# Eight of sixteen ff2 chunks in seven half products, with part of the weight sums made in memory

## The chip, the core and the metric

The kernel runs on one core of a Trainium2 chip. TensorE (PE in the profile; PEld is its weight load) multiplies into PSUM, VectorE (DVE) and ScalarE (ACT) do elementwise work on SBUF and PSUM, GpSimd (POOL) does little here, and SyncE (SP) issues nearly all loads from memory. Each engine works through its own queue in order and waits on semaphores for what others make. The metric is the device time of one execution in microseconds, as the median of some runs.

## The reference

One decoder layer on a sequence of 256 tokens of 1024 channels, in float32. What matters here is its second half:

```python
mixed = g_nsa * (y_nsa @ w_up_nsa[layer]) + g_moba * (y_moba @ w_up_moba[layer])
x = x + mixed @ w_out[layer]                 # 1024 x 1024

h2 = rmsnorm(x, norm2_g[layer])
u = jax.nn.relu(h2 @ w_ff1[layer])           # 1024 x 4096
x = x + (u * u) @ w_ff2[layer]               # 4096 x 1024
return rmsnorm(x, norm_f_g)
```

Ahead of it stand a norm, one wide input projection and two attention mixers.

## The kernel before

**Chunks and slots.** All weights are cut into 60 chunks of up to 1 MB (128 rows of 2048 floats), in the list CHUNKS: kva/kvb (0 to 3), q, qm, km, vm (4 to 11), gm (12 to 19), upn and upm (20 to 23), wout (24 to 27), ff1 (28 to 43), ff2 (44 to 59). The kernel goes through them in slots, one for each chunk. A slot is a list of matmuls with other engines' work put at places in it: `at(pos, f, ...)` notes f at a share of the slot, and `run_slot` calls it ahead of the matmul at that share. So a place only sets the order in which instructions enter their queues; when one runs is up to its engine's queue and to its data.

**Two halves of every number.** Products are made in a fast format, so every operand is split into a rounded part (hi) and a rest (lo), and a product is three matmuls: hi by hi, hi by lo, lo by hi (`mm3`). `split` makes both halves of a weight chunk: ACT copies to hi (L114), DVE subtracts for lo (L116). It runs two slots ahead of its use; loads (`load`, L95) run up to five ahead into three raw buffers, and each waits until the last reader of its buffer's former chunk is done. There are also three hi and three lo buffers, so a chunk's hi waits until PE is through with the slot three chunks before.

**wout.** Each slot makes two blocks of 128 output channels from eight input blocks k (`two_blocks`, 48 matmuls of 256 columns). In the first slot the inputs k = 4 to 7 come late: `mix_t` transposes them on PE into a bank of PSUM, ACT copies them to mxh (L746), `mix_l` lets DVE make mxl (L750). So the slot first does k = 0 to 3 for both blocks, then 4 to 7, always three matmuls for one k.

**ff1.** Sixteen slots of the same form. `ff1_evac` takes a slot's result from PSUM: relu on ACT, the square on DVE (L937), its rounded copy on ACT (L938) and the rest on DVE (L939), into sqh and sql.

**ff2.** Chunk i has the weights of 256 of the 4096 inner channels (two blocks k) for all 1024 outputs. A plain slot is 24 matmuls of 512 columns: two halves of the tokens (t), two blocks k, two halves of the outputs, three matmuls each, added up in four banks of PSUM (`ops`). The chunks in SEVEN (2, 4, 6, 8, 10, 12) are done in the manner of Strassen and Winograd: as 2 by 2 blocks, with seven products in place of eight, 21 matmuls (`seven_mms`). That needs sums of blocks: of the activations (`s_sums`, `s_split`, in ff1) and of the weights (`t_sums`, four subtractions on DVE in place in the raw buffer, L913; then `t_hi`, L920, and `t_lo`, L924, which split the four sums T). Products that enter several outputs (P1, P5, P6, P7) have banks of their own, and `seven_sum` adds them into x1 in the last slots. `x1_rows` turns the layer's residual from columns to rows with 16 transposes on PE, in ff2's slot 1. The last slot does chunks 14 and 15 and puts out the result by `final_a` and `final_b`.

**Queues.** SP issues all loads in the order of the calls. POOL has sixteen small operations at the start, up to the norm's power (L229, L230), and two at the very end (L1048); it issues no transfer.

Of the kernel before, what the change touches and what calls it, by code (L numbers as in the profile page):

```python
# [41 lines left out]
def hybrid_layer(ctx: ExitStack, tc: tile.TileContext, firstd, gxd, w, w1c, small, const, gf, out):  # L42
# [59 lines left out]
    def split(c, part, parts=2, which=""):  # L102
        if c >= NCH:
            return
        n = CHUNKS[c][2]
# [4 lines left out]
        if seven(c):  # L110
            a, b = ((0, 512), (1024, 2048))[part]
        v = raw[c][:, a:b] if c else raw0[:, part]
        if which != "l":
            act.activation(hi[c][:, a:b], v, AF.Copy)  # L114
        if which != "h":
            dve.tensor_tensor(lo[c][:, a:b], v, hi[c][:, a:b].bitcast(F32),  # L116
                              op=ALU.subtract)
# [4 lines left out]
    for _ in range(7):  # L122
        pe.matmul(warm[:, 0:128], zero, zero, start=True, stop=True, skip_group_check=True)
    ident = cp.tile([128, 128], F32, name="ident")
    make_identity(nc, ident)
# [517 lines left out]
    for sec, c0, n in groups:  # L643
# [244 lines left out]
    def s_sums(i, r):  # L888
        if not SS:
            FB["p"].tile([128, 40], F32, name="gap3")  # L890
            for n, e in (("h", 128), ("l", 16)):
                SS[n] = cp.tile([128, 2048 + e], F32R, name="s" + n, tag="act" + n.upper())
                SS[n + "x"] = FB["p"].tile([128, 384], F32R, name="sx" + n)
        j = SEVEN.index(i)
        for n in "hl":
            SS[i, n] = (SS[n][:, 16 + 384 * j:400 + 384 * j] if j < 5 else SS[n + "x"])
# [2 lines left out]
        for o, x, y, op in ((0, A[1][0], A[1][1], ALU.add), (2, A[0][0], A[1][0], ALU.subtract),
                            (1, S[0], A[0][0], ALU.subtract), (3, A[0][1], S[1], ALU.subtract)):  # L900
            dve.tensor_tensor(S[o], x, y, op=op)
# [7 lines left out]
    def t_sums(c):  # L909

        b = raw[c].rearrange("p (a n) -> p a n", a=4)
        for o, x, y in ((0, 1, 0), (1, 3, 1), (3, 3, 0), (2, 2, 3)):
            dve.tensor_tensor(b[:, o], b[:, x], b[:, y], op=ALU.subtract)  # L913

    def t_hi(c, a):
        if a == 0:
            for n in "hl":
                TT[n] = FB["p"].tile([128, 2176 if n == "h" else 2096], F32R, name="t" + n, tag="h2" + n)[:, 0:2048]
        v = slice(1024 * a, 1024 * a + 1024)
        act.activation(TT["h"][:, v], raw[c][:, v], AF.Copy)  # L920

    def t_lo(c, a):
        v = slice(1024 * a, 1024 * a + 1024)
        dve.tensor_tensor(TT["l"][:, v], raw[c][:, v], TT["h"][:, v].bitcast(F32),  # L924
                          op=ALU.subtract)


    def ff1_evac(i, outs, whole):
# [6 lines left out]
        else:  # L935
            act.activation(rf, whole, AF.Relu)
        dve.tensor_tensor(rf, rf, rf, op=ALU.mult)  # L937
        act.activation(h, rf, AF.Copy)  # L938
# [65 lines left out]
    def seven_sum():  # L1004

        s1 = scr[:, 0:512]
        u2, u3 = (FB["p"].tile([128, 2, 256], F32, name="ur", bufs=2)
                  .rearrange("p a q -> p (a q)") for _ in range(2))
        r0, r1 = fst[:, 4:5], fst[:, 5:6]
        add = lambda o, v, r: dve.scalar_tensor_tensor(o, v, r, o, op0=ALU.mult, op1=ALU.add)  # L1010
        act.activation(s1, PP["P1"], AF.Copy)
        dve.tensor_tensor(u2, PP["P6"], s1, op=ALU.add)
        dve.tensor_tensor(u3, PP["P7"], u2, op=ALU.add)
        add(x1[:, 0, 0:512], s1, r0)
        add(x1[:, 0, 512:1024], u2, r0)
        add(x1[:, 0, 512:1024], PP["P5"], r0)
        add(x1[:, 1].rearrange("p (a n) -> p a n", a=2),
            u3[:, None, :].to_broadcast([128, 2, 512]), r1)
        add(x1[:, 1, 512:1024], PP["P5"], r1)

# [43 lines left out]
    for i in range(15):  # L1064
        c = C_FF2 + i
        if i == 13:
            split_events(c, (0.0, 0.1), (0.1, 0.2))
            at(0.45, seven_sum)
        else:
            std_events(c)  # L1070
        for f, a in prev:
            at(0.02, f, *a)
        prev = []
        if i + 2 in SEVEN:
            at(0.62, t_sums, c + 2)
            at(0.65, t_hi, c + 2, 0)
            at(0.66, t_hi, c + 2, 1)
        if i + 1 in SEVEN:
            for a in range(2):
                at(0.03, t_lo, c + 1, a)  # L1080
            at(0.04, load, c + 4)
# [112 lines left out]
```

## Time and profile before

| what | value |
|---|---|
| three runs | 376.36, 376.53, 376.57 us; median 376.53 |
| the profiled execution's own time | 376.16 us |
| its span, first to last instruction | 374.2 us |
| granted TensorE clock, mean | 0.996 |
| DVE's weight splits (L116), 124 of them | 136.3 us busy |
| ACT's weight splits (L114), 124 of them | 118.7 us busy |
| DVE's sums of weight blocks (L913), 24 of 128x512 | 16.6 us busy, 690 ns each |
| DVE's rests of these sums (L924), 12 of 128x1024 | 14.6 us busy, 1221 ns each |
| ff loads, 32 of 1024 KB | 4.9 us from issue to landing (median) |

The profile is of one execution. Its page lists for each engine the busy time, the chain of work that ended last, groups of like instructions (busy time, mean duration in ns, idle time before them and who ended it) and the loads. Matmuls overlap, so the mean duration of one is longer than the spacing between two. The span leaves out 1.96 us of the execution's time, at its start and end.

### The profile page before, as it was taken

The page shows a single profiled execution, that of the slowest core. Times are in us where ns is not written, and L with a number is a line of the kernel's source. Part 1 is how long each engine was busy: PE and PEld are TensorE (multiplying, and loading weights), DVE is VectorE, ACT ScalarE, POOL GpSimd, SP SyncE. Part 2 cuts the span into 40 slices and gives each one's busy share as a digit, 9 for nine tenths or more (in the row PEclk, how much of TensorE's full clock was granted, in tenths as well). Part 3 has the DMA queues.
Part 4 walks back from the last instruction along what each step waited for, and adds up shares of the span by engine and source line. Part 5 has one row for each costly group of instructions (what it writes and reads, how often), then busy time and mean ns, then how long its engine had stood idle before and what let it go on. Part 6 is the DMA issues. An engine that isn't in the chain of part 4 may idle for free.

```text
span 374.2 us, 6013 instructions
## 1 busy us (share of the span) xinstructions
PE 365.3 (98%) x2388; PEld 321.1 (86%) x2388; DVE 295.5 (79%) x476; ACT 220.0 (59%) x382; POOL 6.6 (2%) x18
## 2 busy tenths in 40 slices
PE   8989999999999999999999999999999999999993
PEld 8977778878888788778999999999998888888883
DVE  5878888896966869766867688787778879999685
ACT  6876465767747667344455566766664785555412
POOL 3020000000000000000000000000000000000000
PEclk9999999999999999999999999999999999999998
DMA  7996445334533335550675656456655535655202
GB/s 244 394 412 228 134 177 205 112 114 126 194 130 115 112 119 200 152 203 2 222 286 176 200 190 213 158 192 226 207 160 198 207 131 165 234 199 202 99 0 112
DMA packets 11259, 66.89 MB, mean 179 GB/s; under 512 B 1248, under 2 KB 2272, under 8 KB 3936
## 3 DMA queue, kind: packets, MB, share of 16 engines
q1 hardware_dynamic: 10800, 65.61, 50.1%
q10 hardware_dynamic: 432, 0.92, 0.7%
q8 instruction: 18, 0.29, 0.3%
q14 instruction: 9, 0.07, 0.1%
HBM read 65.47 MB, written 1.05 MB: 178 GB/s over the span
## 4 chain that ended last, share of the span: by engine, by line
PE 83%; DVE 7%; ACT 3%; DMA 3%; issue 2%; SPq 1%; POOL 1%; POOLq 0%; ACTq 0%; DVEq 0%
PE acc L253 53%; PE o L253 13%; PE P L253 4%; PE qacc L253 3%; PE yb L253 2%; DVE wlo L116 2%; DMA raw<-in_kvb_dram 2%; ACT whi L114 2%; DMA g0x<-in_first_dram 1%; DVE x L1010 1%; PE Sa L551 1%; PE Sb L551 1%; PE Sa L253 1%; PE Sb L253 1%; PE tp L341 1%
## 5 line engine op out<-in xcount | busy, mean ns | idle before, releaser
L114 ACT ACTIVATE whi<-raw 128x1024 fp32r<-128x1024 f32 (+3 forms) x124 | 118.7, 984 | 53.3 <-PE acc L253 33.8
L116 DVE TENSOR_TENSOR wlo<-raw,whi 128x1024 fp32r<-128x1024 f32 (+3 forms) x124 | 136.3, 1130 | 13.1 <-ACT whi L114 13.0
L253 PE MATMUL acc<-h2h,whi 128*128 128x256 f32 x256 | 70.7, 276 | 0.0
L253 PE MATMUL acc<-h2l,whi 128*128 128x256 f32 x256 | 70.7, 276 | 0.0
L253 PE MATMUL acc<-h2h,wlo 128*128 128x256 f32 x256 | 70.7, 276 | 0.0
L253 PE MATMUL acc<-whi,hTh 128*128 128x512 f32 (+1 forms) x128 | 50.4, 399 | 0.5 <-ACT whi L114 0.3
L253 PE MATMUL acc<-wlo,hTh 128*128 128x512 f32 (+1 forms) x128 | 49.7, 393 | 0.0
L253 PE MATMUL acc<-whi,hTl 128*128 128x512 f32 (+1 forms) x128 | 49.1, 389 | 0.0
L253 PEld LDWEIGHTS acc<-h2h,whi 128*128 128x128 f32 x256 | 48.0, 188 | 0.0
L253 PEld LDWEIGHTS acc<-h2l,whi 128*128 128x128 f32 x256 | 48.0, 188 | 0.0
L253 PEld LDWEIGHTS acc<-h2h,wlo 128*128 128x128 f32 x256 | 48.0, 188 | 0.0
L253 PE MATMUL o<-whi,sqh 128*128 128x512 f32 (+1 forms) x86 | 33.1, 385 | 0.0
L253 PE MATMUL o<-whi,sql 128*128 128x512 f32 (+1 forms) x86 | 33.0, 384 | 0.0
L253 PE MATMUL o<-wlo,sqh 128*128 128x512 f32 (+1 forms) x86 | 33.0, 384 | 0.0
L253 PEld LDWEIGHTS acc<-whi,hTh 128*128 128x128 f32 x128 | 24.1, 190 | 6.9 <-issue 1.3
L253 PEld LDWEIGHTS acc<-whi,hTl 128*128 128x128 f32 x128 | 24.3, 190 | 4.3
L253 PEld LDWEIGHTS acc<-wlo,hTh 128*128 128x128 f32 x128 | 24.3, 190 | 3.8
L920 ACT ACTIVATE th<-raw 128x1024 fp32r<-128x1024 f32 x12 | 12.8, 1063 | 19.2 <-DVE raw L913 19.2
L939 DVE TENSOR_TENSOR sql<-ur,sqh 128x512 fp32r<-128x512 f32 x16 | 11.1, 692 | 11.2 <-ACT sqh L938 11.2
L253 PEld LDWEIGHTS o<-whi,sql 128*128 128x128 f32 x86 | 16.2, 188 | 3.2
L253 PEld LDWEIGHTS o<-wlo,sqh 128*128 128x128 f32 x86 | 16.1, 188 | 3.2
L253 PEld LDWEIGHTS o<-whi,sqh 128*128 128x128 f32 x86 | 16.2, 188 | 3.1
(319 smaller groups left out, 643.1 us busy)
## 6 DMA issues: line engine op xcount, KB each, us to landing
raw<-in_ff_dram SPq DMA_DIRECT2D x32, 1024.0 KB, 4.9
raw<-in_gm_dram SPq DMA_DIRECT2D x8, 1024.0 KB, 4.8
raw<-in_wout_dram SPq DMA_DIRECT2D x4, 1024.0 KB, 5.0
raw<-in_q_dram SPq DMA_DIRECT2D x2, 1024.0 KB, 7.2
raw<-in_qm_dram SPq DMA_DIRECT2D x2, 1024.0 KB, 7.5
raw<-in_km_dram SPq DMA_DIRECT2D x2, 1024.0 KB, 5.6
raw<-in_vm_dram SPq DMA_DIRECT2D x2, 1024.0 KB, 4.9
raw<-in_upn_dram SPq DMA_DIRECT2D x2, 1024.0 KB, 4.9
```

Of the source, the lines that this page charges most:

```text
L114: act.activation(hi[c][:, a:b], v, AF.Copy)
L116: dve.tensor_tensor(lo[c][:, a:b], v, hi[c][:, a:b].bitcast(F32), op=ALU.subtract)
L253: pe.matmul(o, l, r, start=start, stop=stop, skip_group_check=True)
L341: pe.transpose(tp[:, j * 256 + t * 128:j * 256 + t * 128 + 128], src[:, t, (2 * i + j) * 128:(2 * i + j + 1) * 128], ident)
L551: pe.transpose(S[x][:, j, c:c + 128], P[:, 2 * x + j, c:c + 128], ident)
L920: act.activation(TT["h"][:, v], raw[c][:, v], AF.Copy)
L939: dve.tensor_tensor(l, rf, h.bitcast(F32), op=ALU.subtract)
L1010: add = lambda o, v, r: dve.scalar_tensor_tensor(o, v, r, o, op0=ALU.mult, op1=ALU.add)
```

## The change

- SEVEN becomes (1, 2, 4, 5, 7, 8, 10, 11): eight chunks, in four pairs of neighbours with a plain one between pairs.
- The blocks of these chunks' weights are stored in another order, so that the three blocks that are used as they are (B) are the first 1536 columns; only these are loaded by `load`, 768 KB.
- Of the four weight sums T, two are now made in memory: POOL issues for each such chunk a copy of two blocks into a tile in memory (`v_copy`) and a transfer that adds the fourth block to both (`v_add`), noted in slots 7 to 22 at 0.6. `v_load` (SP, 512 KB) brings the two sums into SBUF, into two buffers vv. DVE makes the other two with two additions (`t_sums`).
- T's hi and lo have one buffer for all of ff2. `t_hi` and `t_lo` of a second chunk of a pair fill its first half at 0.72 of the first chunk's slot, its second half at the start of their own slot.
- The products run in the order P1, C11, C12, P5, P7, P6, C21 (P5, P7, P6, C21 first before).
- Loads of ff2, splits and sums get new places; `seven_sum` is cut in two, in slots 12 and 13; `x1_rows` moves to ff1's slot 3 and uses ff2's four banks.
- In `ff1_evac` ACT makes both squares, and DVE's multiplication goes.
- In wout's first slot (`kinds`), k = 4 to 7 are done kind by kind: all hi by hi, all lo by hi, then all hi by lo. The second `mix_t` there moves from 0.29 to 0.25.

```diff
-SEVEN = (2, 4, 6, 8, 10, 12)
+SEVEN = (1, 2, 4, 5, 7, 8, 10, 11)
...
     def load_part(c, i, parts, m=1):
         sec, j, n = CHUNKS[c]
+        n = 1536 if seven(c) else n
...
+    def v_copy(i):
+
+        VD[i] = dp.tile([128, 1024], F32, name=f"vd{i}")
+        b = w["ff2"][i].rearrange("p (a n) -> p a n", a=4)
+        pool.dma_start(VD[i].rearrange("p (a n) -> p a n", a=2), b[:, 0:3:2, :])
+
+    def v_add(i):
+        b = w["ff2"][i].rearrange("p (a n) -> p a n", a=4)
+        pool.dma_start(VD[i].rearrange("p (a n) -> p a n", a=2),
+                       b[:, 3:4, :].to_broadcast([128, 2, 512]), accum_op=ALU.add)
+
+    def v_load(i):
+        VS[i] = FB["p"].tile([128, 1024], F32, name="vv", bufs=2)
+        nc.sync.dma_start(VS[i], VD[i])
...
+    def v_events(c):
+
+        j = c - 7
+        if 0 <= j < 2 * len(SEVEN):
+            at(0.6, (v_copy, v_add)[j % 2], SEVEN[j // 2])
...
-                mms += wstat(outs[m], c, m * 128, 8, 256, ah, al, ks=ks, last=7)
+                if not (kinds and ks[0]):
+                    mms += wstat(outs[m], c, m * 128, 8, 256, ah, al, ks=ks, last=7)
+        if kinds:
+            for w, x, end in ((hi, ah, 8), (lo, ah, 8), (hi, al, 7)):
+                for m in range(2):
+                    for k in range(late, 8):
+                        mms.append(lambda o=outs[m], w=w[c][:, k * 256 + m * 128:k * 256 + m * 128 + 128],
+                                   x=x[:, k, :], z=k == end: mm(o, w, x, False, z))
...
-            at(0.29, lambda: mix_t(1, 1, s_tile(1)[:, 0]))
+            at(0.25, lambda: mix_t(1, 1, s_tile(1)[:, 0]))
...
-        b = raw[c].rearrange("p (a n) -> p a n", a=4)
-        for o, x, y in ((0, 1, 0), (1, 3, 1), (3, 3, 0), (2, 2, 3)):
-            dve.tensor_tensor(b[:, o], b[:, x], b[:, y], op=ALU.subtract)
+        b = raw[c][:, 0:2048].rearrange("p (a n) -> p a n", a=4)
+        dve.tensor_tensor(b[:, 2], b[:, 2], VS[c - C_FF2][:, 0:512], op=ALU.add)
+        dve.tensor_tensor(b[:, 1], b[:, 1], b[:, 2], op=ALU.add)
+
+    def t_src(c, a):
+        return raw[c][:, 512:1536] if a else VS[c - C_FF2]
...
-        dve.tensor_tensor(rf, rf, rf, op=ALU.mult)
-        act.activation(h, rf, AF.Copy)
+        act.activation(h, rf, AF.Square)
+        act.activation(rf, rf, AF.Square)
         dve.tensor_tensor(l, rf, h.bitcast(F32), op=ALU.subtract)
...
+        if i == 3:
+            at(0.5, x1_rows, range(4), [FB["o"].tile([128, 512], F32, name=f"o{t}_{a}")
+                                        for t in range(2) for a in (0, 512)])
+        if i in (9, 11):
+            at(0.6, v_load, SEVEN[(i - 9) // 2])
...
-        for name, a, b in (("P5", S[0], T[0]), ("P7", S[2], T[1]), ("P6", S[1], T[3]),
-                           ("C21", sq(1, 1), T[2]), ("P1", sq(0, 0), B[0]),
-                           ("C11", sq(0, 1), B[2]), ("C12", S[3], B[3])):
+        for name, a, b in (("P1", sq(0, 0), B[0]), ("C11", sq(0, 1), B[1]), ("C12", S[3], B[2]),
+                           ("P5", S[0], T[0]), ("P7", S[2], T[1]), ("P6", S[1], T[3]),
+                           ("C21", sq(1, 1), T[2])):
...
+        S0, S1, S2 = (i + k in SEVEN for k in range(3))
         if i == 13:
             split_events(c, (0.0, 0.1), (0.1, 0.2))
-            at(0.45, seven_sum)
+        elif S0:
+            split_events(c, *(((0.1, 0.45), (0.4, 9)) if S1 else ((0.4, 0.5), (0.5, 0.6))))
         else:
-            std_events(c)
+            split_events(c, (0.3, 0.45), (0.4, 0.5))
+        if S0:
+            at(0.0, t_hi, c, 1)
+            at(0.01, t_lo, c, 1)
+            at(0.03, load, c + 3)
+            if not S1:
+                at(0.035, load, c + 4)
+            n = SEVEN.index(i) + 2
+            if n < len(SEVEN):
+                at(0.04, v_load, SEVEN[n])
+        if S1:
+            at(0.2 if S0 else 0.1, t_sums, c + 1)
+            at(0.72 if S0 else 0.15, t_hi, c + 1, 0)
+            at(0.73 if S0 else 0.16, t_lo, c + 1, 0)
+        if i in (SEVEN[-1] + 1, SEVEN[-1] + 2):
+            at(0.5, seven_sum, i - SEVEN[-1] - 1)
         for f, a in prev:
             at(0.02, f, *a)
-        prev = []
...
+        prev = [(split, (c + 2, 1, 2, "l"))] if S0 and S1 else []
...
-        if i == 1:
-            at(0.5, x1_rows, range(4), [acc_tile() for _ in range(3)] + [bank("yb", "yb")])
...
+    for i in SEVEN:
+        d["ff2"][i] = d["ff2"][i].reshape(128, 4, 512)[:, [0, 2, 3, 1]].reshape(128, 2048)
```

More of the change, by code (lines that the diff above doesn't have):

```diff
@@ L110, in split @@
         if seven(c):
-            a, b = ((0, 512), (1024, 2048))[part]
+            a, b = ((0, 512), (512, 1536))[part]
         v = raw[c][:, a:b] if c else raw0[:, part]
@@ L297, in split_events @@
                 at(ls[i], split, c + 2, i, 2, "l")
-        if ls[1] <= 1 and not seven(c + 2):
+        if ls[1] <= 1 and not seven(c + 2) and not seven(c + 1):
             at(max(ls) + 0.05, load, c + 5)
@@ L665, in hybrid_layer @@
             unit_events(c)
+            v_events(c)
             if c == 5:
@@ L780, in hybrid_layer, with two_blocks @@
             prev = [(evac, (1, i, accs[1]))]
-    def two_blocks(c, ah, al, late=8):
+    def two_blocks(c, ah, al, late=8, kinds=False):
         if late < 8:
@@ L868, in hybrid_layer @@
         else:
-            mms, outs, _ = two_blocks(c, mxh, mxl, 4 if i == 0 else 8)
+            mms, outs, _ = two_blocks(c, mxh, mxl, 4 if i == 0 else 8, i == 0)
             run_slot(mms)
@@ L892, in s_sums @@
                 SS[n] = cp.tile([128, 2048 + e], F32R, name="s" + n, tag="act" + n.upper())
[L893 removed]
+                SS[n + "x"] = FB["p"].tile([128, 384 * (len(SEVEN) - 5)], F32R, name="sx" + n)
         j = SEVEN.index(i)
         for n in "hl":
[L896 removed]
+            SS[i, n] = (SS[n][:, 16 + 384 * j:400 + 384 * j] if j < 5 else
+                        SS[n + "x"][:, 384 * (j - 5):384 * (j - 4)])
         S = [FB["scr"][:, 128 * a:128 * a + 128] for a in range(4)]
         A = [[r[:, k, 128 * t:128 * t + 128] for k in range(2)] for t in range(2)]
[L899 to L900 removed]
+        for o, x, y, op in ((0, A[1][0], A[1][1], ALU.subtract), (2, A[0][0], A[1][0], ALU.subtract),
+                            (1, S[0], A[0][0], ALU.subtract), (3, A[0][1], S[1], ALU.add)):
             dve.tensor_tensor(S[o], x, y, op=op)
@@ L909, in t_sums @@
     def t_sums(c):
-        b = raw[c].rearrange("p (a n) -> p a n", a=4)
-        for o, x, y in ((0, 1, 0), (1, 3, 1), (3, 3, 0), (2, 2, 3)):
-            dve.tensor_tensor(b[:, o], b[:, x], b[:, y], op=ALU.subtract)
+        b = raw[c][:, 0:2048].rearrange("p (a n) -> p a n", a=4)
[3 more added lines that the diff above has]
+        return raw[c][:, 512:1536] if a else VS[c - C_FF2]
     def t_hi(c, a):
-        if a == 0:
+        if not TT:
             for n in "hl":
                 TT[n] = FB["p"].tile([128, 2176 if n == "h" else 2096], F32R, name="t" + n, tag="h2" + n)[:, 0:2048]
-        v = slice(1024 * a, 1024 * a + 1024)
-        act.activation(TT["h"][:, v], raw[c][:, v], AF.Copy)
+        act.activation(TT["h"][:, 1024 * a:1024 * a + 1024], t_src(c, a), AF.Copy)
     def t_lo(c, a):
         v = slice(1024 * a, 1024 * a + 1024)
-        dve.tensor_tensor(TT["l"][:, v], raw[c][:, v], TT["h"][:, v].bitcast(F32),
+        dve.tensor_tensor(TT["l"][:, v], t_src(c, a), TT["h"][:, v].bitcast(F32),
                           op=ALU.subtract)
@@ L1002, in seven_mms, with seven_sum @@
         return r
-    def seven_sum():
+    UU = {}
+    def seven_sum(t):
+        add = lambda o, v, r: dve.scalar_tensor_tensor(o, v, r, o, op0=ALU.mult, op1=ALU.add)
         s1 = scr[:, 0:512]
[L1007 to L1019, printed above, removed]
+        if t == 0:
+            UU[2], UU[3] = (FB["p"].tile([128, 2, 256], F32, name="ur", bufs=2)
+                            .rearrange("p a q -> p (a q)") for _ in range(2))
+            act.activation(s1, PP["P1"], AF.Copy)
+            dve.tensor_tensor(UU[2], PP["P6"], s1, op=ALU.add)
+            dve.tensor_tensor(UU[3], PP["P7"], UU[2], op=ALU.add)
+            dve.tensor_tensor(UU[2], PP["P5"], UU[2], op=ALU.subtract)
+            add(x1[:, 0, 0:512], s1, fst[:, 4:5])
+            add(x1[:, 0, 512:1024], UU[2], fst[:, 4:5])
+        else:
+            add(x1[:, 1, 0:512], UU[3], fst[:, 5:6])
+            dve.tensor_tensor(UU[3], PP["P5"], UU[3], op=ALU.subtract)
+            add(x1[:, 1, 512:1024], UU[3], fst[:, 5:6])
     def final_a(p, j):
@@ L1065, in hybrid_layer @@
         c = C_FF2 + i
+        S0, S1, S2 = (i + k in SEVEN for k in range(3))
         if i == 13:
             split_events(c, (0.0, 0.1), (0.1, 0.2))
-            at(0.45, seven_sum)
-        else:
-            std_events(c)
+        elif S0:
+            split_events(c, *(((0.1, 0.45), (0.4, 9)) if S1 else ((0.4, 0.5), (0.5, 0.6))))
+        else:
+            split_events(c, (0.3, 0.45), (0.4, 0.5))
[14 more added lines that the diff above has]
+            at(0.5, seven_sum, i - SEVEN[-1] - 1)
         for f, a in prev:
             at(0.02, f, *a)
-        prev = []
[L1074 to L1081, printed above, removed]
+        prev = [(split, (c + 2, 1, 2, "l"))] if S0 and S1 else []
         if i == SEVEN[0]:
```

6 lines of the change are left out of this document (5 added, 1 removed).

## The prediction

> **What bounds the kernel now.** I read the page's busy shares first, then the chain of work that ended last, then the waits of PE, then busy time by stretch.
>
> ```profile
> span 374.2 us, 6013 instructions
> PE 365.3 (98%) x2388; PEld 321.1 (86%) x2388; DVE 295.5 (79%) x476; ACT 220.0 (59%) x382; POOL 6.6 (2%) x18
> PE 83%; DVE 7%; ACT 3%; DMA 3%; issue 2%; SPq 1%; POOL 1%; POOLq 0%; ACTq 0%; DVEq 0%
> ...
> PE yb L123 <- PEq L1178: 0.8, 1, 0.8
> PE tp L253 <- DVE xsq L222: 0.7, 1, 0.7
> PE acc L253 <- ACT whi L114: 0.3, 1, 0.3
> PE tp L388 <- ACT kcd L318: 0.3, 1, 0.3
> PE yb L742 <- DVE sga L735: 0.3, 1, 0.3
> PE acc L253 <- DVE kml L360: 0.2, 1, 0.2
> PE acc L253 <- DVE mxl L750: 0.2, 1, 0.2
> ...
> 177.00:283.00 106.00, 106.00 (x936) 106.00 (x936) 83.24 (x124) 63.51 (x89) 0.00 (x0) 1.00 0.60 204
> 283.00:356.00 73.00, 73.00 (x332) 60.67 (x331) 62.63 (x71) 43.29 (x51) 0.00 (x0) 1.00 0.49 173
> ```
>
> PE holds 83% of the chain, and its seven waits come to 2.8 us in all. The two stretches (columns: length, busy time of PE, PEld, DVE, ACT, POOL, granted clock, DMA share, GB/s) hold three of the four wout slots, the ff1 stage and the ff2 stage to its last slot: PE never pauses there and its clock is full. So in these stages one matmul less is its full price less, as long as DVE (86% in the second stretch), ACT and the loads still deliver in time.
>
> The price of a matmul is not its mean duration:
>
> ```profile
> L253 PE MATMUL o<-whi,sqh 128*128 128x512 f32 x82 | 32.0, 390 | 0.0
> ...
> 176.81 106.25 PE acc L253 x935
> ...
> 299.13 6.80 PE o L253 x30
> ```
>
> By the groups one 512-column matmul lasts 390 ns; by the chain, 30 of them take 6.80 us, so one starts every 0.2267 us; the 256-column ones follow each other at 106.25/935 = 0.1136 us. I take the spacing. [...]
>
> **The change, part by part.**
>
> *Eight chunks instead of six.* A plain ff2 chunk is 24 matmuls, a seven chunk 21. Two more seven chunks remove 6 x 0.2267 = 1.36 us of PE, in the second stretch, where nothing hides them. Moving the 16 transposes of x1_rows from ff2 slot 1 to ff1 slot 3 costs PE the same in either place: 0.
>
> *wout's first slot by kinds.* One wait of PE lies there:
>
> ```profile
> 176.38 0.28 PE L253 MATMUL acc<-mxh,whi 128*128 128x256 f32 x1
> 176.81 0.39 PE L253 MATMUL acc<-mxl,whi 128*128 128x256 f32 x1 [0.15 <-DVE mxl L750]
> 177.03 0.28 PE L253 MATMUL acc<-mxh,wlo 128*128 128x256 f32 x1
> ...
> 175.43 0.60 ACT L746 ACTIVATE mxh<-Sb 128x512 fp32r<-128x512 f32 x1
> 176.06 0.69 DVE L750 SCALAR_TENSOR_TENSOR mxl<-Sb,mxh 128x512 fp32r<-128x512 f32 x1 [0.87 <-ACT mxh L746]
> ```
>
> The first late matmul needs only mxh (there at 176.03) and starts on time; the next needs mxl, which ends at 176.75. Starts are 0.43 and 0.22 us apart where 0.113 is normal: 0.32 + 0.11 = 0.43 us lost, of which I take 0.42. By kinds, sixteen matmuls that need no mxl come first (16 x 0.1136 = 1.8 us), so the first reader of mxl stands at about 178.2, 1.4 us after mxl is ready. mix_t's second call is put two matmuls of 48 earlier; mxh still follows the ACT split before it (174.37 to 175.42), so it is not earlier and need not be. Gain 0.42 us. PE is then that much ahead of DVE, whose next work is the wlo of wout's second slot: from 176.75, 2.35 us (two such splits, in a row below), first half ready at 177.9, second at 179.1. That slot starts at 176.38 + 24 x 0.1136 = 179.1 and reads the second half twelve matmuls in, at 180.5: no new wait.
>
> *ff1's evacuation.* DVE's multiplication goes, ACT gets a second square:
>
> ```profile
> L937 DVE TENSOR_TENSOR ur<-ur 128x512 f32<-128x512 f32 x16 | 11.0, 690 | 7.7 <-ACT ur L936 6.7 <-ACT ur L934 1.0
> L938 ACT ACTIVATE sqh<-ur 128x512 fp32r<-128x512 f32 x16 | 10.1, 633 | 14.7 <-DVE ur L937 14.7
> L906 ACT ACTIVATE sh<-fscr 128x384 fp32r<-128x384 f32 x5 | 2.6, 527 | 1.8 <-DVE fscr L901 1.8
> L906 ACT ACTIVATE sqh<-fscr 128x128 fp32r<-128x128 f32 x6 | 1.9, 311 | 0.4
> ```
>
> A 512-wide ACT operation takes 0.63 here, and I price relu, squares and row copies alike by it. An ff1 slot on PE is 48 x 0.1136 = 5.45 us. ACT has two splits (1.99, in the next fence) + 3 x 0.63 + 0.31 + 0.53 (s_split) = 4.7 us. Slot 3 also gets four row copies (2.5): ACT runs some 1.8 us late there, and its splits are made two slots ahead of PE. Cost 0; without that lead it would be those 1.8 us, once. The two more s_sums and s_splits lie on DVE and ACT in slots with room: 0.
>
> *ff2 in pairs.* Seven chunks now come as (1,2), (4,5), (7,8), (10,11), with one lasting buffer for the T blocks. The rows for DVE and ACT:
>
> ```profile
> 286.18 1.82 DVE L116 TENSOR_TENSOR wlo<-raw,whi 128x512 fp32r<-128x512 f32 x2
> 287.92 2.86 DVE L913 TENSOR_TENSOR raw<-raw 128x512 f32<-128x512 f32 x4
> 290.69 2.44 DVE L924 TENSOR_TENSOR tl<-raw,th 128x1024 fp32r<-128x1024 f32 x2
> 293.05 2.35 DVE L116 TENSOR_TENSOR wlo<-raw,whi 128x1024 fp32r<-128x1024 f32 x2
> ...
> 289.36 1.06 ACT L920 ACTIVATE th<-raw 128x1024 fp32r<-128x1024 f32 x1 [2.87 <-DVE raw L913]
> 291.78 1.99 ACT L114 ACTIVATE whi<-raw 128x1024 fp32r<-128x1024 f32 x2
> ```
>
> Before, two slots (10.2 us of PE) hold 1.82 + 2.86 + 2.44 + 2.35 = 9.47 us of DVE, 93%. After, t_sums has two operations (1.43) instead of four; a group of three slots (2 x 4.76 + 5.44 = 14.96 us) holds 2 x (1.82 + 1.43 + 2.44) + 2.35 = 13.7 us, 92%. No tighter on the mean, so order decides. I count from the start of a pair's first slot, products at 3 x 0.2267 = 0.68 us each in the new order P1, C11, C12, P5, P7, P6, C21. The second chunk's first T half overwrites what P5 and P7 read, so ACT's t_hi waits for P7's end at 3.4 (and the matmul's own length, some 0.2): it runs 3.6 to 4.7, t_lo on DVE 4.7 to 5.9. The second slot's P5 reads it at 4.76 + 2.04 = 6.8: 0.9 us spare. The other half waits for C21 (4.9), is ready at about 7.2, and P6 reads it at 8.2: 1.0 spare. Queued on DVE ahead of them are t_lo (1.2), t_sums (1.4) and a split (1.1), over by about 3.6. In the first pair, where DVE still has the last ff1 evacuation, t_lo ends at about 6.5 against 6.8: 0.2 to 0.3 spare, the tightest place. At the end, seven_sum's first half (five 512-wide operations of 0.69, 3.5 us of DVE) now stands ahead of the last chunk's lo split; by the same count that split ends some 0.9 us before its reader. Cost 0; a miss in any of these places costs PE what it is late by.
>
> *Loads.* A seven chunk now brings 768 KB and 512 KB of sums' parts instead of 1 MB.
>
> ```profile
> raw<-in_ff_dram SPq DMA_DIRECT2D x32, 1024.0 KB, 4.9
> q1 hardware_dynamic: 10800, 65.61, 50.1%
> ...
> raw<-in_ff_dram SPq DMA_DIRECT2D x1, 1024.0 KB, 6.8
> ```
>
> The queue's packets carried 65.61 MB in 50.1% of the span, 350 GB/s. A group of three slots needs 3.67 MB, 10.5 us of its 14.96. The critical transfer is the sums' part issued in a pair's second slot behind 768 KB and 1 MB: the two raw buffers are freed by DVE some 2.6 and 3.7 us into that slot (t_lo's end, then one split), 2.36 MB then take 6.7 us after about 1.9 of start (4.9 less 3.0), so it lands 11.2 us after that slot's start, 1.0 us into the next pair's first slot (4.76 + 5.44 later). t_sums would start then anyway. DVE has about 1.1 us of idle time before t_lo, and P5 0.8 more: it may be 1.9 us late at no cost. The last row is a load issued at 308.41 with none before it in the queue: 1.9 us over the median.
>
> *Side copies.* Sixteen transfers between places in memory on POOL's queue. No row of before shows such a transfer; see the second rival. Here: 0, bounds 0 and 3.2.
>
> ```profile
> 370.62 0.35 ACTq L1056 DMA_DIRECT2D out_dram<-gx  x1
> out_dram<-gx ACTq DMA_DIRECT2D x2, 192.0 KB, 2.7
> ```
>
> *Closing.* The last store is issued at 370.62 and lands 2.7 later; the span ends 0.9 after that, on waits for the queues. A new queue adds to these: between 0 and 0.9, I take 0.1, nearest to nothing since those waits are short ones in a row.
>
> **Sum.** -1.36 - 0.42 + 0.1 = -1.68 us. The profiled execution took 376.16 us (span 374.2), so 374.48 for one like it; the median of the three runs is 376.53, so **374.85 us**.
>
> **Rivals.**
>
> *The sums' part is late.* For: it is the third in its queue, and single loads do land 1.9 us late. Against: this is just the spare time. Each microsecond beyond costs one in each of three pairs (chunks 5, 8, 11). Between 0.5 us once and 0.5 us three times with the tight first pair missed: 375.3 to 376.6.
>
> *The copies run early.* Nothing on POOL stands between the last row of the norm and the end, and the copies wait for nothing but each other, so their place in slots 7 to 22 doesn't hold them:
>
> ```profile
> 22.21 0.55 POOL L230 TENSOR_SCALAR stat<-rstd 128x2 f32<-128x2 f32 x1
> 364.44 0.56 POOL L1048 TENSOR_TENSOR fst<-fst,mhalf 128x1 f32<-128x1 f32 x1 [341.68 <-DVE fst L1041]
> ...
> 27.88 2.01 ACT L114 ACTIVATE whi<-raw 128x1024 fp32r<-128x1024 f32 x2 [1.07 <-DMA raw<-in_qm_dram]
> 30.47 0.22 ACT L408 ACTIVATE hid<-tp 128x64 f32<-128x64 f32 x1 [0.58 <-PE tp L253]
> 31.92 0.45 PE L253 MATMUL tp<-ident,hid 128*64 128x64 f32 x4
> ```
>
> They would start at 22.8, when the qm loads are the latest of all: ACT waits for one until 27.88, the hid copy stands behind it, and PE reads hid at 31.92. That leaves 31.92 - 0.05 - 0.22 - 2.01 - 27.88 = 1.76 us; beyond, PE waits one for one. 512 KB at 350 GB/s is 1.5 us, or 3.0 if reading and writing count apart: 0 or 1.2 us, 374.85 to 376.1. Against: at 1.5 us a copy fits the spare time. A copy that held the loads up for as long as a whole 1 MB load takes (4.9) would cost 3.2: 378.0, slower than before. It decides from a hold-up of 4.2 us (1.76 + 1.68 + 0.75). [...]
>
> *The change doesn't do what it says in wout.* If mxl's reader still waits, or the wait moves to mxh, only 1.36 - 0.1 is left: 375.3.
>
> **How the numbers follow.** A measurement of this kernel tells some 0.2% (0.75 us) from no change: below 375.78 is faster, above 377.28 slower. Forecast (374.5 to 375.2) 55%; sums' part late 15% (most of it faster, a quarter same); copies early at a price that shows 20% (375.2 to 378: a third faster, a quarter same, the rest slower); wout wait stays 10%, faster. Faster 0.83, same 0.09, slower 0.08. The range runs from 374.4 (no closing cost, some noise) to 376.4, which leaves out the copies' upper half and the worst late parts, together under 2 in 10.
>
> **What would show it.** Right: 6 PE matmuls fewer; 512-column ones still 0.2267 us apart with no wait of PE in ff2; the row for mxl gone from PE's waits; ff1 and ff2 together 1.36 us shorter from their first matmul to their last. Wrong: waits of PE on tl, on raw's sums or on whi in slots 2, 5, 8 or 11; ACT waiting for in_qm beyond 29.6; POOL's transfers beside the loads before 40 us with PE idle at hid.

## The result, and the profile after

| | before | after |
|---|---|---|
| median of six runs each, us | 376.57 (376.36 to 378.06) | 375.0 (374.48 to 375.23) |
| ratio, 95% interval | 1 | 0.9947 (0.9929 to 0.9965) |
| the profiled execution, us; its span | 376.16; 374.2 | 374.87; 373.1 |

By the two medians 1.57 us are gone (0.42%); the ratio, which goes with the interval, puts it at 0.53%. 374.85 us was forecast. First the page of the kernel after (span, busy shares, chain of work), then the waits of PE and busy time by stretch, as they were shown of before.

```profile
span 373.1 us, 6063 instructions
PE 364.0 (98%) x2382; PEld 320.5 (86%) x2382; DVE 285.8 (77%) x469; ACT 234.4 (63%) x406; POOL 19.7 (5%) x34
PE 86%; DVE 4%; DMA 3%; issue 2%; ACT 2%; SPq 1%; POOL 1%; POOLq 0%; ACTq 0%
```

```profile
PE tp L272 <- DVE xsq L241: 0.9, 1, 0.9
PE yb L125 <- PEq L1233: 0.8, 1, 0.8
PE acc L272 <- ACT whi L116: 0.3, 1, 0.3
PE tp L407 <- ACT kcd L337: 0.3, 1, 0.3
PE yb L769 <- DVE sga L762: 0.3, 1, 0.3
PE acc L272 <- DVE kml L379: 0.2, 1, 0.2
```

```profile
177.00:285.00 108.00, 108.00 (x954) 107.99 (x954) 76.85 (x122) 75.93 (x113) 0.00 (x0) 1.00 0.59 205
285.00:355.00 70.00, 70.00 (x310) 58.01 (x309) 60.34 (x67) 45.44 (x52) 0.00 (x0) 1.00 0.57 203
```

PE has six matmuls fewer (2388 to 2382), the row for mxl is gone from its waits, and from wout on it still never pauses at a full clock. DVE did 9.7 us less, ACT 14.4 us more, POOL has its sixteen transfers; none of these shows in PE's waits.

Where the time went is read from the starts of PE's matmuls at the borders of the stages: qacc's first, then wout's first (mxh), ff1's first (h2h), ff2's first (sqh) and the last one. PE's timeline of before, then of after:

```profile
24.86 0.40 PE L253 MATMUL qacc<-whi,hTh 128*128 128x512 f32 x1
...
172.73 0.28 PE L253 MATMUL acc<-mxh,whi 128*128 128x256 f32 x1
...
195.85 0.28 PE L253 MATMUL acc<-h2h,whi 128*128 128x256 f32 x1
...
282.89 0.39 PE L253 MATMUL o<-whi,sqh 128*128 128x512 f32 x1
...
367.68 0.28 PE L253 MATMUL yb<-whi,sql 128*128 128x256 f32 x1
```

```profile
25.42 0.40 PE L272 MATMUL qacc<-whi,hTh 128*128 128x512 f32 x1
...
173.30 0.28 PE L272 MATMUL acc<-mxh,whi 128*128 128x256 f32 x1
...
195.99 0.28 PE L272 MATMUL acc<-h2h,whi 128*128 128x256 f32 x1
...
284.80 0.39 PE L272 MATMUL o<-whi,sqh 128*128 128x512 f32 x1
...
366.44 0.28 PE L272 MATMUL yb<-whi,sql 128*128 128x256 f32 x1
```

The differences between neighbours give the stages. The table has them for the one profiled execution of every run below too, worked out from the trace's unrounded starts; the tail is from the last matmul to the span's end.

| run | qacc starts at | to wout | wout | ff1 | ff2 | tail | span |
|---|---|---|---|---|---|---|---|
| before | 24.86 | 147.87 | 23.13 | 87.04 | 84.79 | 6.55 | 374.2 |
| after | 25.42 | 147.88 | 22.69 | 88.81 | 81.65 | 6.63 | 373.1 |
| e1_kinds | 25.28 | 147.83 | 22.69 | 87.04 | 84.79 | 6.54 | 374.2 |
| e2_nokinds | 25.43 | 147.87 | 23.13 | 88.81 | 81.65 | 6.62 | 373.5 |
| e3_six | 25.26 | 147.86 | 22.69 | 88.81 | 83.01 | 6.80 | 374.4 |
| e4_nocopies | 25.10 | 147.86 | 22.69 | 88.81 | 81.65 | 6.55 | 372.7 |
| e5_pad512 | 25.13 | 147.88 | 22.69 | 88.81 | 82.73 | 7.06 | 374.3 |
| e6_pad1024 | 25.28 | 147.83 | 22.69 | 88.81 | 87.32 | 7.08 | 379.0 |
| e7_first | 25.21 | 149.21 | 22.69 | 88.81 | 81.65 | 6.62 | 374.2 |
| e8_nine | 26.71 | 147.85 | 22.69 | 88.81 | 83.31 | 6.66 | 376.0 |
| e9_nine13 | 25.29 | 147.87 | 22.69 | 88.81 | 81.15 | 7.90 | 373.7 |
| e10_dvemult | 25.10 | 147.85 | 22.69 | 88.81 | 81.65 | 6.62 | 372.7 |
| e11_nine_late | 26.60 | 147.86 | 22.69 | 88.81 | 82.95 | 6.83 | 375.7 |
| e12_nine_order | 25.14 | 147.85 | 22.69 | 88.81 | 81.07 | 6.57 | 372.1 |

From before to after: wout -0.43, ff1 and ff2 together -1.37 (x1_rows took 1.77 us from ff2 to ff1), tail +0.08, and qacc's start +0.56. That last one is there before POOL issues its first transfer at 23.27, and it differs by 0.3 to 0.4 us among runs that are the same up to there (25.10 to 25.43 in those like after, 24.86 and 25.28 in before and e1). So nothing shows it to be a part of the change; what sets it stays open. Behind qacc's start a stage that a run didn't change repeats to 0.05 us, from wout to ff2 to 0.01, so the table can tell apart what the medians, with intervals of 0.3 to 0.5%, cannot.

### The profile page after: what moved, and what is told of

The parts are those of the page before. It is cut to its first block, busy times and chain, and to the rows that moved or that the text cites. A ratio compares the mean times of both kernels' runs of the same rounds, so it can differ in the third digit from the quotient of the medians.

```text
span 373.1 us, 6063 instructions
## 1 busy us (share of the span) xinstructions
PE 364.0 (98%) x2382; PEld 320.5 (86%) x2382; DVE 285.8 (77%) x469; ACT 234.4 (63%) x406; POOL 19.7 (5%) x34
## 4 chain that ended last, share of the span: by engine, by line
PE 86%; DVE 4%; DMA 3%; issue 2%; ACT 2%; SPq 1%; POOL 1%; POOLq 0%; ACTq 0%
PE acc L272 53%; PE o L272 15%; PE P L272 6%; PE qacc L272 3%; PE yb L272 2%; DVE wlo L118 2%; DMA raw<-in_kvb_dram 2%; DMA g0x<-in_first_dram 1%; PE Sa L570 1%; PE Sb L570 1%; PE Sa L272 1%; PE Sb L272 1%; ACT whi L116 1%; PE tp L360 1%; PE tp L272 1%
## 5 line engine op out<-in xcount | busy, mean ns | idle before, releaser
L272 PE MATMUL o<-whi,sql 128*128 128x512 f32 (+1 forms) x72 | 27.6, 384 | 0.0
L272 PE MATMUL o<-wlo,sqh 128*128 128x512 f32 (+1 forms) x72 | 27.6, 384 | 0.0
L272 PE MATMUL o<-whi,sqh 128*128 128x512 f32 (+1 forms) x72 | 27.6, 384 | 0.0
L272 PE MATMUL acc<-mxh,wlo 128*128 128x256 f32 x64 | 16.7, 278 | 0.0
L272 PE MATMUL acc<-mxh,whi 128*128 128x256 f32 x64 | 16.7, 278 | 0.0
L272 PE MATMUL acc<-mxl,whi 128*128 128x256 f32 x64 | 16.5, 277 | 0.0
L272 PEld LDWEIGHTS o<-whi,sql 128*128 128x128 f32 x72 | 13.5, 188 | 2.7
```

The costliest lines, as they stand in the source:

```text
L272: pe.matmul(o, l, r, start=start, stop=stop, skip_group_check=True)
```

## The experiments

Times are medians of runs beside the kernel before on the same chip, in brackets the ratio to it with its 95% interval.

**The parts one by one: e1_kinds, e2_nokinds, e3_six, e10_dvemult.** e1 puts the third part alone into before:

```diff
-            mms, outs, _ = two_blocks(c, mxh, mxl, 4 if i == 0 else 8)
+            mms, outs, _ = two_blocks(c, mxh, mxl, 4 if i == 0 else 8, i == 0)
```

(with `kinds` in two_blocks and the second mix_t at 0.25).

> The kernel before with the third part of the change alone: wout's first slot runs all hi products of k 4 to 7, then lo, then the mxl ones, and mix_t of the second group stands at 0.25 of its slot. Theory (the prediction's second step): the 0.42 us that TensorE waits for mxl in that slot goes and nothing takes its place, so the time is 0.42 us under before (376.1 on the scale of 376.5), and the stretch from wout's first matmul to ff1's first goes from 23.13 to 22.70 us. Rival: the wait only moves to the evacuation or to the next slot, stretch 23.1, time as before.

e2 takes the same lines out of after.

> The kernel after without the third part: wout's first slot in the old order, mix_t back at 0.29. Theory: only the wout stretch changes, 22.69 back to 23.12 us, so 0.43 us over after, 375.4. Rival (the parts are not independent, the copies on POOL's queue or the loads shift with it): another size, or none.

e3 takes two chunks out of after, `SEVEN = (1, 2, 4, 5, 7, 8)`.

> The kernel after with seven products in six chunks (1, 2, 4, 5, 7, 8) instead of eight; the making of the sums in memory stays, for six chunks. Theory (the prediction's first step): six 512-column matmuls more at 0.2267 us, so 1.36 us over after, 376.3, and the stretch from ff1's first to the last matmul goes from 170.45 to 171.81. Rival A (the sums' parts that land at 2.1 us into a slot cost TensorE something in each pair): under 1.36, as one pair's cost goes with its gain. Rival B (the gain is from the new layout of a chunk and not from the count of chunks): close to 0.

e10 gives ff1's evacuation back to DVE:

```diff
-        act.activation(h, rf, AF.Square)
-        act.activation(rf, rf, AF.Square)
+        dve.tensor_tensor(rf, rf, rf, op=ALU.mult)
+        act.activation(h, rf, AF.Copy)
```

> The kernel after with the squares of ff1's evacuation back where they were: VectorE multiplies, ScalarE copies the rounded part. Theory (the move was costed at nothing because neither engine ends a wait of TensorE in ff1): 0 in every stretch, within 0.05 us. Rival (VectorE needs that time in ff1, as s_sums and the split come behind the evacuation): TensorE waits in ff1's slots or at the first pair, up to 0.7 us for each of 8 slots with sums.

Measured: e1 376.7 (0.9995, 0.9979 to 1.001), e2 375.12 (0.9949, 0.993 to 0.9968), e3 376.16 (0.9987, 0.9969 to 1.0005), e10 375.07 (0.9956, 0.9941 to 0.9971). By the medians e1 and e2 are misses: e1 is 0.14 us over before where 0.42 under it were expected, e2 0.12 over after where 0.43 were expected, though the intervals hold both. The stages settle it: wout is 22.69 with the new order and 23.13 without, in before and in after alike, and nothing behind it moves. In the two profiled executions e1's start is 0.42 us later than before's, which hides just this gain. In e3 ff2 is 1.36 us longer, to the hundredth what six matmuls at 0.2267 us cost, and its tail 0.17 (two more of SP's closing waits, 0.06 us each, stand behind the last store's landing). In e10 no stage differs from after's: DVE's 11 us of multiplications in ff1 were hidden, so ACT's taking them over brought nothing by itself. wout's order is worth the same in both kernels, so the parts add up.

**The copies: e4_nocopies, e7_first.** e4 issues none and loads each part straight from the chunk's first 1024 columns, so the sums of weights are left out:

```diff
-        nc.sync.dma_start(VS[i], VD[i])
+        nc.sync.dma_start(VS[i], w["ff2"][i][:, 0:1024])
...
-            at(0.6, (v_copy, v_add)[j % 2], SEVEN[j // 2])
+            pass
```

> The kernel after without the 16 transfers that make the sums in memory: each part is loaded straight from the ff2 chunk's first 1024 columns, so the weights' sums are left out of the computation. Theory (the prediction's costs of the copies: nothing while they run, 0.1 us of closing waits at the end): 0.1 us under after, 374.9, with the tail from the last matmul back at 6.55 from 6.63. Rival (the copies cost TensorE or the startup something that the walk didn't see: the start of the first qacc matmul is 0.57 us later in after than in before): 0.6 us or more under after, with the qacc start back at 24.9 from 25.4.

e7 issues all eight copies at once, then the eight adding transfers:

```diff
-        if 0 <= j < 2 * len(SEVEN):
-            at(0.6, (v_copy, v_add)[j % 2], SEVEN[j // 2])
+        if j == 0:
+            for i in SEVEN:
+                at(0.6, v_copy, i)
+            for i in SEVEN:
+                at(0.6, v_add, i)
```

> The kernel after with all eight copies in memory issued one after the other by POOL from about 22.8 us, and the eight adding transfers behind them, instead of one in each slot. The prediction's second rival (the copies hold up the qm loads; 1.76 us spare there; decides from 4.2 us) gives 2.5 us over after, about 377.5, with qm0 landing at 32 us instead of 27.8 and TensorE waiting for it. The theory that the copies take so little from the loads that nothing is reached: within 0.2 us of after, qm0 within 1 us of 27.8. In both, the gm loads, which in after took 7.1 instead of 4.8 us beside the copies, show how much the loads lose.

First how the copies ran in after: POOL's timeline, ACT's, and the DMA issues (KB each, us from issue to landing).

```profile
23.27 0.80 POOL L132 DMA_DIRECT2D vd<-in_ff_dram  x1
31.80 1.12 POOL L136 DMA_DIRECT2D vd<-in_ff_dram  x1 [7.73 <-DMA vd<-in_ff_dram]
...
27.85 2.01 ACT L116 ACTIVATE whi<-raw 128x1024 fp32r<-128x1024 f32 x2 [0.48 <-DMA raw<-in_qm_dram]
```

```profile
vd<-in_ff_dram POOLq DMA_DIRECT2D x16, 512.0 KB, 8.8
raw<-in_gm_dram SPq DMA_DIRECT2D x8, 1024.0 KB, 7.1
```

They did start at 23.27, right behind the norm's last row, as the second rival said, and one took 8.8 us, not 1.5 to 3.0. The gm loads beside them took 7.1 us; in e4, with no copies, 5.0. But the loads had that time: qm's split began at 27.85 (27.88 before), and e4 has the same stages as after, only the tail 0.08 shorter. e4 took 374.52 (0.9937, 0.9915 to 0.9959), and its stages are what the first theory expected. By time it is 0.48 us under after's median, which alone would suit the rival, but the two intervals overlap and its start (25.10) lies among the others. In e7 (375.52; 0.9964, 0.9938 to 0.999) both expectations miss on the place: hid is read 7.05 us after qacc's start as in after (7.06), and qm cost nothing. It was the km load, 11.7 us to landing (7.4 in after), that came late: ACT, DVE and PE in e7,

```profile
42.28 1.06 ACT L116 ACTIVATE whi<-raw 128x1024 fp32r<-128x1024 f32 x1 [1.84 <-DMA raw<-in_km_dram]
43.24 0.36 ACT L377 ACTIVATE kwh<-tp 128x256 fp32r<-128x256 f32 x1
43.51 0.27 ACT L378 ACTIVATE kw<-tp 128x128 f32<-128x128 f32 x1
43.80 0.42 DVE L379 TENSOR_TENSOR kwl<-tp,kwh 128x256 fp32r<-128x256 f32 x1 [2.68 <-ACT kw L378]
...
44.28 0.66 PE L360 MATMUL tp<-ident,qtm 128*128 128x128 f32 x4 [1.16 <-DVE kwl L379]
```

two small copies on ACT stand behind a split that waits for its load, and PE waits 1.2 us for what DVE makes of them. The stage is 1.33 us longer (147.88 to 149.21). So the rival's mechanism exists. After and e7 differ in nothing but when the transfers are issued: in after each adding transfer waits for its copy to land (7.73 us in the row above), so at most two are under way at once, and the loads lose less (km 7.4 us against 11.7, qm 7.4 against 8.2).

**How late the sums' parts may be: e5_pad512, e6_pad1024.** An extra load of unused data goes ahead of the part (1024 columns in e5, 2048 in e6):

```diff
+    def pad():
+        nc.sync.dma_start(gx[:, 16:16 + 1024], w["gm"][0][:, 0:1024])
...
             if n < len(SEVEN):
+                if not S1:
+                    at(0.038, pad)
                 at(0.04, v_load, SEVEN[n])
```

> The kernel after with one more 512 KB load of unused data on SP's queue ahead of the sums' part in the second slot of each pair, three of which stand ahead of another pair. A load behind others takes 1.25 to 2.1 us for 512 KB in after's trace. The prediction's figure (a part may come 1.9 us late at no cost): 0 to 0.2 us for each of three pairs, so 0 to 0.5 us over after. By after's own trace (the part lands 2.1 us into its slot, VectorE waits 1.0 to 1.4 us for it, and the P5 product has 0.88 us left): 0.4 to 1.2 us for each, so 1.2 to 3.5 us over after, with TensorE waiting ahead of the P5 products. Rival (TensorE's fp32r products wait on something else and the loads have no part in it): 0.

> The same with 1 MB ahead of the sums' part (2.5 to 4.1 us). The prediction's 1.9 us spare: 0.6 to 2.2 us for each of three pairs, 1.8 to 6.6 us over after. By after's trace (0.88 us spare): 1.6 to 3.2 us for each, 5 to 9.7 us. Whichever holds, this run less the one with 512 KB gives the slope: time over after that grows by 1.25 to 2.1 us for each pair and 512 KB more, once the spare is gone.

In after, the first sum of chunk 5 waits for its part vv, then its tl stands ready for the product P5, whose second matmul is the first to read it (DVE's and PE's timeline; [1.04 <- ...] is the idle time before a row and what ended it):

```profile
307.40 0.69 DVE L948 TENSOR_TENSOR raw<-raw,vv 128x512 f32<-128x512 f32 x1 [1.04 <-DMA vv<-vd]
...
309.90 1.23 DVE L962 TENSOR_TENSOR tl<-vv,th 128x1024 fp32r<-128x1024 f32 x1
...
322.32 0.69 DVE L948 TENSOR_TENSOR raw<-raw,vv 128x512 f32<-128x512 f32 x1 [1.43 <-DMA vv<-vd]
...
337.24 0.69 DVE L948 TENSOR_TENSOR raw<-raw,vv 128x512 f32<-128x512 f32 x1 [1.37 <-DMA vv<-vd]
...
312.01 0.39 PE L272 MATMUL P<-th,sqh 128*128 128x512 f32 x1
312.24 0.39 PE L272 MATMUL P<-tl,sqh 128*128 128x512 f32 x1
```

tl ends at 311.13, its reader starts at 312.24: 1.11 us spare, and DVE's waiting for vv leaves no more than that. In e5, then in e6, the same three sums start as follows (and last a row of e6's view of PE's waits: total, times, longest):

```profile
307.94 0.69 DVE L951 TENSOR_TENSOR raw<-raw,vv 128x512 f32<-128x512 f32 x1 [1.91 <-DMA vv<-vd]
...
323.36 0.69 DVE L951 TENSOR_TENSOR raw<-raw,vv 128x512 f32<-128x512 f32 x1 [2.19 <-DMA vv<-vd]
...
339.05 0.69 DVE L951 TENSOR_TENSOR raw<-raw,vv 128x512 f32<-128x512 f32 x1 [2.54 <-DMA vv<-vd]
```

```profile
309.59 0.69 DVE L951 TENSOR_TENSOR raw<-raw,vv 128x512 f32<-128x512 f32 x1 [3.43 <-DMA vv<-vd]
...
326.74 0.69 DVE L951 TENSOR_TENSOR raw<-raw,vv 128x512 f32<-128x512 f32 x1 [3.90 <-DMA vv<-vd]
...
343.77 0.69 DVE L951 TENSOR_TENSOR raw<-raw,vv 128x512 f32<-128x512 f32 x1 [3.88 <-DMA vv<-vd]
```

```profile
PE P L275 <- DVE tl L965: 4.8, 3, 1.9
```

e5's ff2 starts 0.28 us earlier than after's, so its parts are later than after's by 0.82, 1.32 and 2.09 us (307.94 + 0.28 - 307.40, and so on). Less 1.11 of spare, and less what PE has already waited: 0, 0.21 and 0.77, 0.98 in all; ff2 is 1.08 us longer. The same sum for e6 (0.18 earlier) gives 1.26, 2.23 and 2.11, 5.60 in all; ff2 is 5.67 us longer. (The row's 4.8 is less, as it counts from the end of the matmul before.) The spare is 1.1 us, not 1.9. In ff2, e5 falls between the two expectations (1.08; 0.5 and 1.2 were the nearest ends), because its first pair still fits into the spare; with its longer tail (1.52 in all) it lies in the second. e6 lies in both. From e5 to e6 a pair pays 1.53 us for 512 KB, in the expected 1.25 to 2.1, though the first pair still had spare left in e5. (Medians: e5 376.2; 0.9979, 0.9953 to 1.0004. e6 380.84; 1.0126, 1.011 to 1.0142. Their tails are 0.44 us longer too: DVE reaches the last bank's addition 0.12 us later, and seven of SP's closing waits stand behind the last store's landing, where after has two.)

**A ninth chunk: e8_nine, e9_nine13, e11_nine_late, e12_nine_order.** If six matmuls less are worth 1.36 us, three more should be worth 0.68. e8 makes groups of three:

```diff
-SEVEN = (1, 2, 4, 5, 7, 8, 10, 11)
+SEVEN = (1, 2, 3, 5, 6, 7, 9, 10, 11)
```

(the final norm's gain loads later and lends its place to the ninth chunk's sums; the copies begin a slot earlier).

> The kernel after with nine chunks of seven products (1 to 3, 5 to 7, 9 to 11) in groups of three instead of eight in pairs; the norm's gain loads in ff2's slot 12, its place being used for the ninth chunk's sums. Theory (each chunk of seven saves three matmuls, 0.68 us, as long as VectorE and the loads keep up): 0.68 us under after, 374.3. Rival (VectorE and the queue are at their limit: by after's trace a part lands 2.1 us into its slot with 0.88 us left, and in a group of three the part has one slot less to come): TensorE waits at each third chunk, 1 to 2 us for each of three groups, so 2 to 5 us over after.

Measured 377.81 (1.0017, 0.9995 to 1.0039). In the profiled execution (378.2) 1.3 us are the late start; ff2 is 83.31, 1.66 over after. That is the rival, though its waits for tl (0.98, 0.45 and 0.46 us) are shorter than its 1 to 2. DVE and PE of e8 at the first third chunk:

```profile
300.54 0.69 DVE L949 TENSOR_TENSOR raw<-raw,vv 128x512 f32<-128x512 f32 x1 [0.56 <-DMA vv<-vd]
...
301.88 1.22 DVE L118 TENSOR_TENSOR wlo<-raw,whi 128x1024 fp32r<-128x1024 f32 x1
303.01 1.22 DVE L963 TENSOR_TENSOR tl<-vv,th 128x1024 fp32r<-128x1024 f32 x1
...
304.28 0.50 PE L272 MATMUL P<-tl,sqh 128*128 128x512 f32 x1 [0.82 <-DVE tl L963]
```

tl comes 0.98 us late, and ahead of it DVE does a wlo that PE reads only a slot later; the sum before it also waited 0.56 us for its part. Is DVE full, or its queue badly ordered? e9 avoids groups of three, with a ninth chunk alone in slot 13 and the closing sums in the last slot:

```diff
+SEVEN = (1, 2, 4, 5, 7, 8, 10, 11, 13)
...
+        if i == 14:
+            seven_sum(0)
+            at(0.3, seven_sum, 1)
```

(as in e8 the copies begin a slot earlier and the final norm's gain lends its place, here to the first chunk's sums; it loads in slot 2).

> The kernel after with a ninth chunk of seven products, chunk 13 by itself, in place of the groups of three of the earlier run; the closing sums of the half products stand in the last double slot, the first half of them ahead of everything. Theory (pairs and single chunks leave VectorE its time, and the waits in the run with groups of three came from VectorE's two splits ahead of the third chunk's part): three matmuls fewer, 0.68 us under after in the stretch from ff2's first to the last matmul (81.65 to 80.97) with no wait for tl, and 374.3 in time. Rival (the closing sums and the last split now collide with the final additions on VectorE): the last double slot has a wait, or the tail behind the last matmul grows by more than 0.68 us, and the time is after's or over.

Measured 375.8 (0.9977, 0.9955 to 0.9999): the rival again. ff2 is 81.15, 0.5 us under after (of the 0.68 of three matmuls) and with no wait for tl, but the tail grew by 1.27 (0.78 over after in all): DVE reaches the last bank's addition at 367.46, 1.65 us after the last matmul (365.81), in after 0.32 us after it.

e11 goes back to groups of three and puts the untimely split off:

```diff
-            split_events(c, *(((0.1, 0.45), (0.4, 9)) if S1 else ((0.4, 0.5), (0.5, 0.6))))
+            split_events(c, *(((0.1, 0.45 if S2 else 9), (0.4 if S2 else 0.8, 9)) if S1 else ((0.4, 0.5), (0.5, 0.6))))
```

(9 means: with the next slot's first work).

> The run with nine chunks in groups of three (1 to 3, 5 to 7, 9 to 11) once more, with one thing put off: in the middle slot of a group the split of the second next chunk (ScalarE's second half and VectorE's first) comes behind the third chunk's th and tl of the sums' part. Theory (in the earlier run the third chunk waited 0.98, 0.45 and 0.46 us for tl because VectorE did that split of 1.13 us ahead of it): these waits go, the stretch from ff2's first to the last matmul is 80.97 us (81.65 of after less 0.68) and the time 374.3, under both kernels. Rival (VectorE's time in a group of three is used up whatever the order): the split of the second next chunk is then late itself, with TensorE waiting for wlo at the slot behind the group, and the stretch stays over 81.65.

Measured 376.47 (0.9998, 0.9986 to 1.001), ff2 82.95. The waits at the first tl went, but neither theory had it right: PE now waited at the second tl, 0.64, 0.68 and 0.23 us, where that split had been put. e12 moves the rest of it behind, and loads the third chunk's part earlier:

```diff
+            split_events(c, *(((0.1, 0.45), (0.4, 9)) if S1 and S2 else ((0.75, 9), (9, 9)) if S1 else ((0.4, 0.5), (0.5, 0.6))))
...
+                at(0.025 if S1 and S2 else 0.04, v_load, SEVEN[n])
...
+        prev = [(split, (c + 2, 0, 2, "l"))] if S0 and S1 and not S2 else []
+        prev += [(split, (c + 2, 1, 2, "l" if S2 else ""))] if S0 and S1 else []
```

> Nine chunks in groups of three, with the rest of the order mended: in the middle slot of a group all of the second next chunk's split comes behind the third chunk's th and tl, and in the first slot the third chunk's sums' part is loaded ahead of the next chunk. In the run before this one the third chunk's first tl came in time, and TensorE waited 0.64, 0.68 and 0.23 us at the next one, which stood behind one split of 1.22 us; VectorE also stood idle 0.45, 0.51 and 0.71 us for the sums' part. Theory (order alone was in the way): no wait for tl, the stretch from ff2's first to the last matmul 80.97 to 81.1 us, and a time 0.5 to 0.7 us under after. Rival (VectorE's time is used up): the waits move to wlo of the chunk behind each group, 0.3 to 0.7 us each, and the stretch is over 81.65.

Measured 374.47 (0.9939, 0.9915 to 0.9962). The same place in e12:

```profile
299.77 1.22 DVE L964 TENSOR_TENSOR tl<-vv,th 128x1024 fp32r<-128x1024 f32 x1
301.30 1.23 DVE L964 TENSOR_TENSOR tl<-raw,th 128x1024 fp32r<-128x1024 f32 x1 [0.30 <-ACT th L960]
302.44 2.35 DVE L118 TENSOR_TENSOR wlo<-raw,whi 128x1024 fp32r<-128x1024 f32 x2
...
301.73 0.39 PE L272 MATMUL P<-tl,sqh 128*128 128x512 f32 x1
```

No wait for tl or wlo is left in ff2, which takes 81.07 us, 0.57 less than in after. Order alone, DVE's and the loads', was in the way in e8 and in e11. Which of the two counts for more was not tried apart. e12 is under before beyond doubt (the interval ends at 0.9962), and by stages (ff2 and tail) 0.63 us under after; by time, two ratios with overlapping intervals, the two can't be told apart.

## Why the prediction was right, step by step

- **Six matmuls at the spacing, -1.36:** ff1 and ff2 lost 1.37; putting three a chunk back (e3) cost 1.36. The busy mean of 390 ns would have said 6 x 0.390 = 2.34.
- **wout by kinds, -0.42:** 0.43, in after and alone (e1, e2). The third rival, that the wait remains, fell.
- **Closing, +0.1:** 0.08, and gone without POOL's transfers (e4). The size is right, the mechanism not, so that is partly luck: SP ends on nine waits instead of five, but the four more are over before the last store lands. Nearly all of the 0.08 lies between SP's last two instructions, 0.46 us apart instead of 0.39; what makes it stays open.
- **ff1's evacuation, x1_rows, the sums in ff1, 0:** no wait of PE there; e10 shows that the multiplication could have stayed on DVE.
- **ff2 in pairs, 0:** no wait. The second chunk's P5 was to have 0.9 us; it has 0.88 from tl's end to its first matmul, 1.11 to the one that reads tl. In the first pair, the tightest place (0.2 to 0.3), tl ended at 296.59 and P5 began at 297.05: 0.46.
- **Loads, 0:** the price is right, the term behind it mis-sized. The part was to land 1.0 us into the pair's first slot and to have 1.9 us more. It landed at 307.31, and that slot's first product starts at 305.21: 2.1 us in. By the trace its three loads were issued at 297.75, 298.88 and 299.30, within 0.2 us of where the walk had them, but landed at 301.94, 306.06 and 307.31: the last 1.57 MB took 5.37 us, 293 GB/s where I had taken 350, the mean while the queue is busy. DVE's 1.04 us of waiting for it in after is the idle time that was counted as spare, so the first rival was 1.1 us away instead of 1.9; e5 and e6 met it there.
- **Side copies, 0:** right in the sum, wrong in the working. They run early, as the second rival said, and take 8.8 us, three times the upper estimate. What I asked was whether they delay qm, and they don't; the place that pays first, when they are crowded (e7), is km's split. That the term was zero is therefore in part luck. (Its upper bound, 4.9 less 1.76, is 3.1, not 3.2.)
- **Not in the sum:** the start. It was 0.56 us later in after's profile than in before's, so the two profiled executions differ by only 1.29, where the stages behind the start gave 1.72 and 1.68 was forecast. How far it moves the medians, 1.57 apart, the profiles don't show.

## What to carry to other kernels

Where one engine never pauses, price a removed instruction by the spacing of its neighbours (here 1.36 us for six, where 1.37 were measured), and check it stage by stage between fixed instructions: here that resolves 0.05 us where medians resolve 1. The spare time of a transfer is the reader's start less the end of the last step that makes what it reads, and padding the queue measures it. An engine that is 90% busy is not yet full (DVE 91% from 285 to 354 us in e12, with no wait of PE there): see first whether something it does could come later (e8 and e12 do the same work in another order, 2.2 us of ff2 apart).

## What the runs showed of the hardware

**The start's clock.** In all runs PE stands idle for 0.7 to 1.0 us near 19 us, waiting for xsq. In two profiled executions of fourteen (e8, e11) the granted clock fell after it, and qacc began 1.2 to 1.3 us later than in after. Windows of e8 (length, busy PE, PEld, DVE, ACT, POOL, clock, DMA share, GB/s), then its PE timeline:

```profile
20.00:24.00 4.00, 3.70 (x15) 3.69 (x16) 3.47 (x6) 2.96 (x5) 2.55 (x3) 0.65 1.01 422
```

```profile
21.20 0.51 PE L272 MATMUL kvbacc<-whi,hTl 128*128 128x408 f32 x1
21.50 0.55 PE L272 MATMUL kvbacc<-whi,hTh 128*128 128x408 f32 x1
21.84 0.55 PE L272 MATMUL kvbacc<-wlo,hTh 128*128 128x408 f32 x1
```

Matmuls of 408 columns start 0.34 us apart there, 0.19 elsewhere. Over 20 to 24 and 24 to 28 us the granted clock was 0.65 and 0.92 in e8, 0.61 and 0.96 in e11, and 1.00 in both windows in the other twelve. Ahead of the fall PE waited 0.17 us for wlo and 1.01 for xsq in e8, 0.16 and 1.01 in e11. But e4, e5, e9 and e12 have both waits too, 0.2 and 1.0 us, and kept the full clock. So these waits alone don't bring the fall; what does was not shown, and no run moved the waits to try it.

**Transfers between places in memory.** 512 KB issued by POOL took 8.8 us (median of sixteen in after), eight at once 25.1 (median, with the adding ones; e7), while a 768 KB load took 4.3. They slowed SP's loads: gm took 5.0 us in e4, 7.1 in after; km 6.0 in e4, 7.4 in after, 11.7 in e7.
